# A two-layer hybrid trunk: a new table of start and end positions for the 39 streams that its instructions are woven from

## The chip, the cores and the metric

The kernel runs on one core of one Trainium2 chip, as one program from the input arrays in device memory to the output array. The metric is the device time of an execution in microseconds, the median of several runs; less is better. Besides the times there is a trace of one profiled execution, and all views below are of that one.

The engines are named as in the trace: PE is TensorE's matmuls (PEld its weight loads), DVE is VectorE, ACT is ScalarE, POOL is GpSimd, and SP is the engine that issues the weight loads from device memory. Each engine works through its own list of instructions in order, and waits on semaphores where an instruction needs another engine's result.

## The reference

Two layers. Each normalises x, projects it once to all inputs of four branches, runs the branches, gates each with a SiLU, and maps the four outputs back.

```python
for l in range(DEPTH):                       # DEPTH 2, SEQ 1024, D_MODEL 1024
    h = rms_norm(x, pre_norm_g[l])
    proj = h @ w_in[l]
    (a_val, a_glu, a_gate, b_q, b_f, b_i, b_gate,
     c_xbc, c_dt, c_z, d_cq, d_ckv, d_kr, d_gate) = jnp.split(proj, split_at, axis=-1)
    y_a = conformer_conv_branch(a_val, a_glu, a_gate, ...)   # GLU, causal depthwise conv k=31, LN, swish, pointwise
    y_b = hgrn2_branch(b_q, b_f, b_i, b_gate, ...)           # gated linear recurrence
    y_c = ssd_branch(c_xbc, c_dt, c_z, ...)                  # short conv, chunked scan, gated RMSNorm
    y_d = mla_branch(d_cq, d_ckv, d_kr, d_gate, positions, ...)  # low-rank q / kv, rotary, block-causal attention
    y = jnp.concatenate([y_a, y_b, y_c, y_d], axis=-1) @ w_out[l]
    x = x + rms_norm(y, post_norm_g[l])
```

The depthwise convolution of branch A, `y[t] = sum_k w[k] * h[t-30+k]` per channel over 31 taps, and the recurrence of branch B, `state = exp(b_last) * state + k^T v` with decays inside the chunk, are the two that matter here.

## The kernel before, in words

Everything is in one function, `trunk_kernel`. A layer's body creates some twenty generators, one for each piece of work, and emits their instructions interleaved. In the order in which they come in a layer:

- **v** (`th_v`) projects branch B's values: tiles `psV` (and `psVb` for the first two token blocks of layer 1, whose matmuls follow the previous layer's last blocks as they arrive). PE only waits there for the transposed, normalised input `hh`/`hl`.
- **a** (`th_a`) projects branch A's value and GLU gate (`psA`, each 128 features by 1024 tokens), and DVE multiplies them into the padded inputs `hpad` of the convolution (L468, L470).
- **ca** and **cb** (`th_conv`) are the convolution: 240 instructions `ca<-hpad,col,ca` on DVE (L481), 120 in each layer. They need only `hpad`, their result is read much later (`th_atail`), so they can be put almost anywhere between.
- **fq** (`th_fq`) projects forget gate and query of branch B: `psF`, `psQ`.
- **dt** (`th_dt`) makes branch C's step sizes on DVE, two matmuls `pcs`, a transpose `pct`, and a small transfer of POOL's queue, `acsp<-acT` (L448).
- **b** (`th_b`) is branch B's recurrence. For each half `g` of the tokens there are seven levels, and in each level two halves `m`. A half of a level issues four matmuls `plB` (L625) from `krb` and `qz`, then DVE rescales `qz` (L634) and `krb` (L635) for the next level; after both halves two `copy_predicated` (L648) take the level's `plB` out of PSUM into `amat` (the last two levels use ACT instead). A level's `plB` waits for the last level's L634 and L635. After the levels come `poB`, `ptkB`, `pSB`, which carry the state from block to block.
- **gb**, **gc** (`gate`, tiles `psg`) and **ga**, **gd** (`gate_f`, tiles `psgA`) project the SiLU gates of the branches; POOL's queue stores them (`gsp`, `gspF`) and reads them back later (`gl`, `glA`, `gD`).
- **x** (`th_x`, tiles `psx`) projects branch C's input; DVE does its short convolution (L719). **at** is the rest of branch A, **c** branch C's scan (its `lm` is read by POOL's queue from `acsp`, then gets the mask added by DVE at L736), **d** (`psd`) branch D's projections, **q** and **att** its attention (`psc`, `ptp`, `poD`; DVE's maxima `nm`, ACT's exponentials `pe`).
- **w** (`th_w`) loads the output projection's weights: eight transfers `rawo` through two buffers, each split by ACT into `woh` and by DVE into `wol`. `woh` and `wol` take the room of `hh` and `hl`, so the first split waits for the last matmul that reads `hh`, which is a `psd`. **o** and the code behind it do the output projection (`pz`) and the next layer's normalisation.

A weight chunk from device memory goes through two `raw` buffers, is cut by ACT into a rounded `wh` (L160) and by DVE into the rest `wl` (L176), three buffers each; every product is three matmuls (`wh` by `hh`, `wl` by `hh`, `wh` by `hl`).

What sets the order: each generator has a row (start, end, total) in the table `PLAN`, and is a `Thread` whose position is start + (end - start) * done / total. `weave` always takes the next piece from the thread with the lowest position. The instruction lists that come out of this are then ordered once more at build time by the framework's scheduler, which puts ready instructions ahead; the lists shown below under the change are those that result from both. The positions are numbers on a scale of the table's own; a layer's scale runs to about 505.

Of the kernel before, what the change touches and what calls it, by code (L numbers as in the profile page):

```python
# [43 lines left out]

PLAN = {
    "v0": (-1.1, 7.4, 8),
    "a0": (35.1, 68.9, 41),
    "fq0": (60.4, 110.8, 41),
    "dt0": (104, 115.8, 9),
    "ca0": (53.6, 123, 57),  # L50
    "cb0": (123, 300.5, 63),
    "gb0": (138.1, 155.9, 21),
    "b0": (123.3, 232.4, 120),
    "ga0": (151.5, 181.4, 21),
    "gc0": (203.4, 226.9, 21),
    "gd0": (278.8, 298.3, 21),
    "x0": (220.7, 257, 61.5),
    "at0": (296.3, 363.8, 22),
    "c0": (293.2, 362.4, 48.2),
    "d0": (283.6, 373.2, 72),  # L60
    "q0": (357.3, 375.6, 2),
    "o0": (470, 505, 8.2),
    "rot0": (221.2, 266.5, 1),
    "att0": (347.7, 481.2, 144.8),
    "w0": (425, 460, 8),
    "v1": (-3.5, 30.6, 8),
    "a1": (35.1, 68.9, 41),
    "fq1": (59, 99.6, 41),
    "dt1": (104, 115.8, 9),
    "ca1": (57, 110, 44),  # L70
    "cb1": (110, 284.5, 76),
    "gb1": (117.9, 137.7, 21),
    "b1": (102.3, 200.5, 120),
    "ga1": (130.9, 155.3, 21),
    "gc1": (203.4, 230.3, 21),
    "gd1": (261.8, 280.6, 21),
    "x1": (212.9, 255.7, 61.5),
    "at1": (278.6, 342, 22),
    "c1": (275.5, 340.6, 48.2),
    "d1": (266.1, 351.4, 72),  # L80
    "q1": (335.5, 349.5, 2),
    "o1": (468, 503, 8.2),
    "att1": (347.1, 481.6, 144.8),
    "w1": (425, 455, 8),
}


# [1101 lines left out]
```

## Time and profile before

| | |
|---|---|
| median of 3 runs | 1258.37 us (1258.11 to 1260.59) |
| the profiled execution | 1256.95 us, of which its span is 1255.2 us |
| mean granted TensorE clock | 0.985 of full speed |
| busy over the span: PE, PEld, DVE, ACT, POOL | 1196.8, 985.2, 808.7, 488.5, 180.0 us |
| recurrence of layer 0, from the first `plB` to the last eight | 140.0 to 256.9 us of the span |
| recurrence of layer 1, the same | 752.3 to 873.0 us of the span |

A row of the view by stretches gives, for each engine, its busy microseconds and, in brackets, its instructions; then the clock granted to TensorE as a share of full speed, the busy share of the DMA engines and the GB/s. A row of the timeline gives start, duration, engine, line, operation, the tile written and the tiles read, the count of like instructions that are drawn together, and in square brackets the idle time before it with what ended it. Matmuls overlap in the pipeline, so that the distance from start to start is what one costs, not its duration. A granted clock of 1.00 is 2.4 GHz, 0.50 is 1.2 GHz.

### The profile page before, as it was taken

Reading aid. Unit: us, or ns where it says so; the run is one execution under the profiler, and the core shown is the slowest. Engines: PE = TensorE matmul, PEld = TensorE weight load, DVE = VectorE, ACT = ScalarE, POOL = GpSimd, SP = SyncE. Lnnn points to the kernel's source line nnn. Section 1 sums busy time; section 2 is a strip of 40 time slices with the busy share of each in tenths; the row PEclk is TensorE's granted clock in tenths of the full one; section 3 lists DMA queues with packets and bytes.
Section 4 is the critical chain, followed back from the end, with each engine's and each line's share of the span. In section 5 each row is a group of like instructions: output and inputs, shape, how many; then the busy total and the mean of one; then the engine's idle time right before and its main releaser. Section 6 shows DMA issues by size and latency. Waiting matters only on the chain.

```text
span 1255.2 us, 17851 instructions
## 1 busy us (share of the span) xinstructions
PE 1196.8 (95%) x6902; PEld 985.2 (78%) x6902; DVE 808.7 (64%) x1555; ACT 488.5 (39%) x1112; POOL 180.0 (14%) x290
## 2 busy tenths in 40 slices
PE   5999999999989989999999999998999898999997
PEld 5988899888878846677898889897888696567786
DVE  5566999985366575527454859999763775654432
ACT  5413222233456474425432222322344755643311
POOL 2100011101132111211020001211011232011100
PEclk9999999999989999999999999998999999999999
DMA  8002122211142140234321111211013312111532
GB/s 275 34 34 68 43 85 79 71 41 52 54 134 74 40 154 19 73 125 168 104 94 68 34 51 60 86 59 67 34 49 101 118 60 100 49 40 43 176 138 81
DMA packets 38661, 101.48 MB, mean 81 GB/s; under 512 B 5440, under 2 KB 13808, under 8 KB 38576
## 3 DMA queue, kind: packets, MB, share of 16 engines
q1 hardware_dynamic: 22848, 51.42, 12.1%
q0 software_dynamic: 14864, 46.04, 11.0%
q10 hardware_dynamic: 864, 2.88, 0.6%
q8 instruction: 54, 0.88, 0.3%
q14 instruction: 31, 0.25, 0.1%
HBM read 75.37 MB, written 25.20 MB: 80 GB/s over the span
## 4 chain that ended last, share of the span: by engine, by line
PE 76%; DVE 11%; issue 4%; DMA 4%; ACT 3%; POOL 0%; SPq 0%; DVEq 0%; ACTq 0%; POOLq 0%
PE pz L1012 11%; PE psx L220 4%; PE psx L223 4%; PE psx L226 4%; DVE ca L481 3%; PE poD L949 3%; PE psc L926 3%; PE ptp L944 2%; PE plB L625 2%; PE psA L220 2%; PE psA L223 2%; PE psA L226 2%; PE psgA L347 2%; PE psgA L348 2%; PE psgA L349 2%
## 5 line engine op out<-in xcount | busy, mean ns | idle before, releaser
L481 DVE SCALAR_TENSOR_TENSOR ca<-hpad,col,ca 128x512 f32<-128x512 f32 x240 | 186.1, 781 | 4.0
L176 DVE TENSOR_TENSOR wl<-raw,wh 128x1024 fp32r<-128x1024 f32 (+2 forms) x56 | 66.9, 1194 | 95.3 <-ACT wh L160 95.2
L160 ACT CAST wh<-raw 128x1024 fp32r<-128x1024 f32 (+2 forms) x56 | 57.5, 1027 | 141.5 <-PE psA L223 33.7
L1012 PE MATMUL pz<-woh,yh 128*128 128x512 f32 x240 | 76.9, 400 | 1.2 <-ACT yh L160 1.2
L1012 PE MATMUL pz<-woh,yl 128*128 128x512 f32 x240 | 76.6, 398 | 0.2 <-DVE yl L176 0.2
L1012 PE MATMUL pz<-wol,yh 128*128 128x512 f32 x240 | 76.0, 396 | 0.0
L209 PE MATMUL psg<-wh,hh 128*128 128x256 f32 x256 | 73.9, 289 | 1.5 <-ACT gt L160 1.4
L210 PE MATMUL psg<-wl,hh 128*128 128x256 f32 x256 | 73.2, 286 | 0.0
L211 PE MATMUL psg<-wh,hl 128*128 128x256 f32 x256 | 72.8, 284 | 0.0
L625 PE MATMUL plB<-qz,krb 128*128 128x128 f32 x448 | 62.8, 288 | 8.6 <-DVE krb L635 8.6
L625 PEld LDWEIGHTS plB<-qz,krb 128*128 128x128 f32 x448 | 58.0, 199 | 11.0 <-issue 5.1
L933 ACT ACTIVATE pe<-psc,nm 128x1024 f32<-128x1024 f32 (+7 forms) x64 | 47.1, 738 | 42.6 <-DVE nm L928 22.4
L220 PE MATMUL psx<-hh,wh 128*128 128x512 f32 x192 | 62.8, 406 | 0.0
L223 PE MATMUL psx<-hl,wh 128*128 128x512 f32 x192 | 62.2, 403 | 0.0
L226 PE MATMUL psx<-hh,wl 128*128 128x512 f32 x192 | 61.9, 401 | 0.0
L719 DVE SCALAR_TENSOR_TENSOR xbc<-xpad,col,xbc 128x512 f32<-128x512 f32 x72 | 51.1, 748 | 16.3 <-ACT xbc L172 15.5
L926 PE MATMUL psc<-kT,qTt 96*128 96x512 f32 (+4 forms) x128 | 53.4, 544 | 5.7 <-ACT pe L933 3.5
L1012 PEld LDWEIGHTS pz<-wol,yh 128*128 128x128 f32 x240 | 44.9, 188 | 10.3
L1012 PEld LDWEIGHTS pz<-woh,yl 128*128 128x128 f32 x240 | 44.7, 188 | 10.4 <-DVE yl L176 0.6
L1012 PEld LDWEIGHTS pz<-woh,yh 128*128 128x128 f32 x240 | 44.1, 188 | 10.7 <-ACT yh L160 1.4
L348 PE MATMUL psgA<-hl,wh 128*128 128x512 f32 x128 | 51.0, 398 | 0.0
L347 PE MATMUL psgA<-hh,wh 128*128 128x512 f32 x128 | 50.9, 397 | 0.0
(335 smaller groups left out, 3001.2 us busy)
## 6 DMA issues: line engine op xcount, KB each, us to landing
raw<-in_w_dram SPq DMA_DIRECT2D x44, 512.0 KB, 3.4
rawo<-in_wo_dram SPq DMA_DIRECT2D x16, 512.0 KB, 3.5
gsp<-gt POOLq DMA_DIRECT2D x16, 256.0 KB, 2.5
gl<-gsp POOLq DMA_DIRECT2D x8, 512.0 KB, 5.1
gspF<-gtA POOLq DMA_DIRECT2D x16, 256.0 KB, 2.3
ysp<-gl POOLq DMA_DIRECT2D x8, 512.0 KB, 3.4
lm<-acsp POOLq DMA_DIRECT2D x16, 256.0 KB, 4.0
yt<-ysp SPq DMA_DIRECT2D x16, 256.0 KB, 3.4
```

The source lines that it names most:

```text
L209: T.matmul(ps[:, :n], a, hs[k], start=(k == 0), stop=False)
L210: T.matmul(ps[:, :n], a, ls[k], start=False, stop=False)
L211: T.matmul(ps[:, :n], b, hs[k], start=False, stop=(k == KD - 1))
L220: T.matmul(ps[:, h * 512:(h + 1) * 512], w, hh[:, k, h * 512:(h + 1) * 512], start=(k == 0), stop=False)
L223: T.matmul(ps[:, h * 512:(h + 1) * 512], w, hl[:, k, h * 512:(h + 1) * 512], start=False, stop=False)
L226: T.matmul(ps[:, h * 512:(h + 1) * 512], wl, hh[:, k, h * 512:(h + 1) * 512], start=False, stop=(k == KD - 1))
L347: T.matmul(ps, w, hh[:, k, tk], start=(k == 0), stop=False)
L348: T.matmul(ps, w, hl[:, k, tk], start=False, stop=False)
L481: V.scalar_tensor_tensor(t, hp[:, k:k + 512], w[k], t, op0=ALU.mult, op1=ALU.add)
L625: T.matmul(pl[:, o0:o0 + P].rearrange("p (r b u) -> p r b u", r=2, u=u), k_[:, t_ * P:(t_ + 1) * P], z[:, :, t_ * P:(t_ + 1) * P].rearrang ...
L926: T.matmul(psc[:, c0:c1_], qTt[0:k_, 2 * m + r, :], kT[2 * m + r, c0 // 512][0:k_, 0:c1_ - c0], start=True, stop=True)
L1012: T.matmul(pz[n], a[:, k, :], w[:, k, n * 512:(n + 1) * 512], start=(k == 0 and a is yh and w is wh), stop=(k == KD - 1 and a is yl))
```

## The change

Only the table `PLAN` is replaced: all of its 39 rows but `v0` have other numbers. No instruction is added to or taken from any engine but one more load of an ACT table (23 to 24), and SP's transfers come in the same order. Two rows of each layer, as an example:

```diff
-    "cb0": (123, 300.5, 63),
+    "cb0": (131.0, 304.2, 63),
-    "gb0": (138.1, 155.9, 21),
+    "gb0": (120.6, 156.4, 21),
...
-    "v1": (-3.5, 30.6, 8),
+    "v1": (5.7, 44.5, 8),
-    "a1": (35.1, 68.9, 41),
+    "a1": (13.5, 44.9, 41),
-    "dt1": (104, 115.8, 9),
+    "dt1": (116.3, 159.5, 9),
```

What comes out of it, on the engines concerned:

In layer 1, PE's list where the projection of V goes over from its first two blocks (`psVb`) to the others (`psV`); `psA` are the projections of the convolution branch. Before:

```order
L210 MATMUL psVb_5567<-wl_5561,hh1_4858 128x260
L211 MATMUL psVb_5567<-wh_5560,hl1_4859 128x260
L209 MATMUL psV_5676<-wh_5554,hh1_4858 128x260
L210 MATMUL psV_5676<-wl_5555,hh1_4858 128x260
L211 MATMUL psV_5676<-wh_5554,hl1_4859 128x260
```

Now:

```order
L220 MATMUL psA_5633<-hh1_4858,wh_5623 128x512 x2
L223 MATMUL psA_5633<-hl1_4859,wh_5623 128x512 x2
L226 MATMUL psA_5633<-hh1_4858,wl_5624 128x512 x2
L209 MATMUL psV_5765<-wh_5554,hh1_4858 128x260
L210 MATMUL psV_5765<-wl_5555,hh1_4858 128x260
L211 MATMUL psV_5765<-wh_5554,hl1_4859 128x260
```

Pieces of `psA` now stand in six places between those of V, where before all but 11 matmuls of `psA` followed V.

In layer 1, DVE's list in the last but one level of the recurrence's second half (of seven, both halves `m`): `ca` is the convolution, `qz` and `krb` the rescaling on which the next `plB` waits. Before:

```order
L481 SCALAR_TENSOR_TENSOR ca_7447<-hpad_6103,col_5536,ca_7447 128x512
L634 TENSOR_TENSOR qz_7012<-qz_7012,totB_6334 128x16x32
L635 TENSOR_TENSOR krb_6114<-krb_6114,totB_6334 128x8x32
L481 SCALAR_TENSOR_TENSOR ca_6980<-hpad_6100,col_5536,ca_6980 128x512
L481 SCALAR_TENSOR_TENSOR ca_7447<-hpad_6103,col_5536,ca_7447 128x512
L634 TENSOR_TENSOR qz_7035<-qz_7035,totB_6334 128x16x32
L635 TENSOR_TENSOR krb_6258<-krb_6258,totB_6334 128x8x32
```

Now:

```order
L481 SCALAR_TENSOR_TENSOR ca_6987<-hpad_6015,col_5536,ca_6987 128x512
L634 TENSOR_TENSOR qz_6957<-qz_6957,totB_6328 128x16x32
L635 TENSOR_TENSOR krb_6108<-krb_6108,totB_6328 128x8x32
L481 SCALAR_TENSOR_TENSOR ca_6987<-hpad_6015,col_5536,ca_6987 128x512
L634 TENSOR_TENSOR qz_6969<-qz_6969,totB_6328 128x16x32
L635 TENSOR_TENSOR krb_6250<-krb_6250,totB_6328 128x8x32
```

One `ca` stands there now where two stood. Counted over the whole lists, from the recurrence's first L635 to the one on which its last `plB` waits (142.7 to 250.2 us and 754.8 to 866.7 us before): `ca` 59 before and 46 now in layer 1 (39 and 30 ahead of it, 22 and 44 behind it), 53 and 45 in layer 0 (51 and 60 ahead, 16 and 15 behind); `wl` 6 and 4, `prB` 3 and 2, the L607 rows 6 and 4 in each layer; and five small rows of `th_dt` and one of `th_c` (L437, L438, L443, L447, L777) come into it in each layer. On PE, from first to last `plB`: `psg` 384 and 358, `psx` 24 and 2, `dsB` 24 and 32 in layer 0; `psg` 384 and 374, `psx` 19 and 2 in layer 1; `pcs` and `pct` come in.

In layer 1, PE's list at the handover to the attention: the last `psd` (after which `wol` may be written), then the first scores `psc`. Before:

```order
L832 MATMUL psd_9051<-idn_81,cn_9077 128x128 x3
L760 MATMUL pyC_9094<-xdt_9018,lm_8986 128x64 x4
L764 MATMUL pyC_9094<-hst_8200,xbc4_7897 128x128
L764 MATMUL pyC_9094<-hst_8200,xbc5_7966 128x128
L872 MATMUL pq_9114<-qbt_5542,cqT_8050 128x384
L872 MATMUL pq_9114<-qbt_5542,cqT_8051 128x384
L847 MATMUL pk_9153<-kvt_5543,ckT_9090 128x512
L860 MATMUL pk_9133<-idn_81,kk_9135 96x128 x4
L885 MATMUL ptq_9125<-idn_81,qk_9117 96x128 x4
L860 MATMUL pk_9153<-idn_81,kk_9155 96x128 x4
L926 MATMUL psc_9184<-kT_8042,qTt_9040 128x512
```

Now:

```order
L832 MATMUL psd_9089<-idn_81,cn_9115 128x128 x3
L847 MATMUL pk_9133<-kvt_5543,ckT_9017 128x512
L847 MATMUL pk_9153<-kvt_5543,ckT_9128 128x512
L860 MATMUL pk_9133<-idn_81,kk_9135 96x128 x4
L860 MATMUL pk_9153<-idn_81,kk_9155 96x128 x4
L926 MATMUL psc_9184<-kT_8116,qTt_9043 128x512
```

The scan's `pyC` and the queries' `pq` and `ptq` stand ahead of the last `psd` now. In layer 0 it is alike: `pyC`, `pq` and one `ptq` went ahead of it.

On POOL's queue in layer 1, `acsp<-acT` stood ahead of all stores of the gate `gb`; now it stands behind the second store of `gc`, near the recurrence's end, and the first `lm<-acsp` one store behind it. On DVE the mask addition to that `lm` (L736) then comes between the last two L635 of the recurrence.

## Rows read from the trace of the kernel before

**Rows 1.** The page's first section: busy time and share of the span.
```profile
PE 1196.8 (95%) x6902; PEld 985.2 (78%) x6902; DVE 808.7 (64%) x1555; ACT 488.5 (39%) x1112; POOL 180.0 (14%) x290
```

**Rows 2.** View by stretches of 25 us: PE, PEld, DVE, ACT, POOL; clock, DMA.
```profile
100.00:125.00 25.00, 25.00 (x112) 20.41 (x111) 14.66 (x29) 9.35 (x15) 0.00 (x0) 1.00 0.18 63
...
225.00:250.00 25.00, 21.97 (x178) 21.20 (x177) 24.87 (x45) 7.10 (x14) 6.05 (x6) 0.92 0.22 74
...
325.00:350.00 25.00, 25.00 (x112) 20.66 (x111) 6.54 (x9) 10.90 (x17) 4.34 (x8) 1.00 0.25 84
...
850.00:875.00 25.00, 19.44 (x109) 17.23 (x108) 24.96 (x40) 5.67 (x11) 2.86 (x3) 0.80 0.22 75
...
975.00:1000.00 25.00, 20.82 (x133) 17.67 (x132) 17.90 (x62) 19.38 (x64) 6.85 (x12) 1.00 0.40 123
```

**Rows 3.** The same columns for the recurrences, and for the stages beside layer 1's.
```profile
140.00:256.90 116.90, 112.94 (x834) 105.40 (x834) 115.29 (x194) 29.70 (x57) 20.19 (x26) 0.97 0.21 73
142.70:250.20 107.50, 103.54 (x788) 97.40 (x788) 106.27 (x184) 29.70 (x57) 18.31 (x24) 0.98 0.21 74
752.30:873.00 120.70, 113.26 (x830) 105.27 (x830) 118.89 (x200) 29.67 (x58) 20.12 (x25) 0.96 0.19 71
754.80:866.70 111.90, 104.46 (x789) 97.73 (x789) 110.14 (x188) 29.65 (x57) 18.73 (x24) 0.97 0.21 76
...
686.50:754.80 68.30, 68.30 (x312) 55.73 (x311) 47.72 (x84) 16.08 (x23) 0.53 (x1) 1.00 0.14 47
875.00:975.00 100.00, 99.91 (x486) 82.15 (x485) 56.90 (x89) 40.35 (x66) 12.45 (x21) 1.00 0.20 64
```

**Rows 4.** DVE's groups by line in 754.8 to 866.7: count, busy us, mean ns, idle.
```profile
L481 DVE SCALAR_TENSOR_TENSOR ca<-hpad,col,ca 128x512 f32<-128x512 f32 x59 | 45.4, 778 | 0.7
...
L176 DVE TENSOR_TENSOR wl<-raw,wh 128x1024 fp32r<-128x1024 f32 x6 | 7.3, 1213 | 0.0
...
L607 DVE TENSOR_TENSOR qz<-qp,fg 64x512 f32<-64x512 f32 x6 | 4.1, 683 | 0.0
...
L598 DVE TENSOR_TENSOR prB<-qp,krb 128x512 f32<-128x512 f32 x3 | 2.0, 686 | 0.0
```

**Rows 5.** Timeline of PE at the end of layer 1's recurrence.
```profile
859.49 1.34 PE L625 MATMUL plB<-qz,krb 128*128 128x128 f32 x8 [3.45 <-DVE krb L635]
...
869.43 1.05 PE L220 MATMUL psx<-hh,wh 128*128 128x512 f32 x2
...
872.95 1.05 PE L625 MATMUL plB<-qz,krb 128*128 128x128 f32 x8
```

**Rows 6.** Timeline of PE in layer 0's recurrence, two neighbouring gate matmuls.
```profile
206.75 0.28 PE L209 MATMUL psg<-wh,hh 128*128 128x256 f32 x1
206.87 0.28 PE L210 MATMUL psg<-wl,hh 128*128 128x256 f32 x1
```

**Rows 7.** View by stretches: the two handovers to the attention.
```profile
437.20:459.70 22.50, 17.24 (x73) 8.88 (x73) 19.02 (x31) 19.26 (x39) 4.54 (x6) 1.00 0.55 188
1053.50:1075.90 22.40, 17.89 (x62) 9.07 (x61) 17.82 (x31) 18.25 (x38) 4.81 (x6) 0.85 0.49 165
```

**Rows 8.** Timeline of PE at layer 1's handover.
```profile
1053.66 1.00 PE L760 MATMUL pyC<-xdt,lm 128*128 128x64 f32 x8
...
1056.79 1.12 PE L847 MATMUL pk<-kvt,ckT 128*128 128x512 f32 x2 [0.33 <-DVE cqT L160]
...
1062.63 6.59 PE L926 MATMUL psc<-kT,qTt 100*128 100x512 f32 x8 [1.10 <-ACT kT L160]
```

**Rows 9.** What reads `rawo`: count, min/median/max ns, first and last start.
```profile
L176 DVE TENSOR_TENSOR wol<-rawo,woh x8: 1212/1221/1226, 437.2 to 1061.8; 128x1024 fp32r<-128x1024 f32 x8
```

**Rows 10.** Transfers from POOL's queue: count, KB each, median us to landing.
```profile
gsp<-gt POOLq DMA_DIRECT2D x16, 256.0 KB, 2.5
...
gspF<-gtA POOLq DMA_DIRECT2D x16, 256.0 KB, 2.3
...
lm<-acsp POOLq DMA_DIRECT2D x16, 256.0 KB, 4.0
```

More of the change, by code (lines that the diff above doesn't have):

```diff
@@ L46 @@
     "v0": (-1.1, 7.4, 8),
[L47 to L50, printed above, removed]
-    "cb0": (123, 300.5, 63),
-    "gb0": (138.1, 155.9, 21),
[L53 to L58, printed above, removed]
-    "c0": (293.2, 362.4, 48.2),
[L60 to L65, printed above, removed]
-    "v1": (-3.5, 30.6, 8),
-    "a1": (35.1, 68.9, 41),
-    "fq1": (59, 99.6, 41),
-    "dt1": (104, 115.8, 9),
[L70 to L84, printed above, removed]
+    "a0": (34.2, 67.6, 41),
+    "fq0": (104.3, 116.8, 41),
+    "dt0": (124.5, 129.4, 9),
+    "ca0": (56.5, 116.0, 57),
+    "cb0": (131.0, 304.2, 63),
+    "gb0": (120.6, 156.4, 21),
+    "b0": (120.8, 230.5, 120),
+    "ga0": (156.4, 186.3, 21),
+    "gc0": (205.1, 219.6, 21),
+    "gd0": (273.1, 274.1, 21),
+    "x0": (216.6, 270.4, 61.5),
+    "at0": (296.3, 361.6, 22),
+    "c0": (293.2, 362.4, 48.2),
+    "d0": (302.0, 372.7, 72),
+    "q0": (360.0, 385.0, 2),
+    "o0": (474.0, 507.1, 8.2),
+    "rot0": (235.4, 295.8, 1),
+    "att0": (356.5, 493.5, 144.8),
+    "w0": (435.6, 485.6, 8),
+    "v1": (5.7, 44.5, 8),
+    "a1": (13.5, 44.9, 41),
+    "fq1": (51.5, 90.6, 41),
+    "dt1": (116.3, 159.5, 9),
+    "ca1": (54.2, 116.7, 44),
+    "cb1": (116.2, 280.3, 76),
+    "gb1": (117.8, 125.5, 21),
+    "b1": (99.5, 192.9, 120),
+    "ga1": (118.3, 173.6, 21),
+    "gc1": (182.3, 209.6, 21),
+    "gd1": (257.3, 280.3, 21),
+    "x1": (201.8, 233.0, 61.5),
+    "at1": (281.5, 341.5, 22),
+    "c1": (259.4, 326.1, 48.2),
+    "d1": (266.1, 356.4, 72),
+    "q1": (331.2, 342.1, 2),
+    "o1": (462, 503, 8.2),
+    "att1": (352.9, 480.9, 144.8),
+    "w1": (430, 455, 8),
 }
```

## The prediction

> **What bounds the kernel now.** I read the busy shares first, then the span in stretches of 25 us, then each stretch in which PE is idle or its clock is down. PE is busy for 95% of the span [rows 1], so the kernel is PE's, and a new order can only win what PE loses to waits and to half clock. These losses are few and stand together: the ends of both recurrences (225 to 250 us and 850 to 875 us: PE 21.97 and 19.44 of 25 at 0.92 and 0.80 of the clock), the start of branch C's scan (975 to 1000 us: 20.82) [rows 2], and the handovers to the attention (17.24 of 22.5 and 17.89 of 22.4) [rows 7]. The reader is to look at DVE in the same rows: at the ends of the recurrences it is full (24.87 of 25).
>
> So over the recurrences DVE is the bound. From the first `krb` to the one on which the last `plB` waits it is busy 106.27 of 107.5 us in layer 0 and 110.14 of 111.9 us in layer 1 [rows 3]. PE runs ahead while it has gate matmuls to put between, and then stands: at the end of layer 1 it waits 3.45 us for a `krb`, and the matmuls behind that run at half clock: two `psx` of 512 columns take 1.05 us [rows 5], where the stretch 325 to 350 us has 112 matmuls of mostly that size in 25.00 us, 0.223 each [rows 2]. A fall of the clock to 1.2 GHz follows the wait, so the wait is paid twice.
>
> **The change, part by part.**
>
> *DVE in the recurrences.* Between the same two `krb`, layer 1 loses 13 `ca` at 0.778, 2 `wl` at 1.213, one `prB` at 0.686 and 2 L607 at 0.683 [rows 4]: 10.1 + 2.4 + 0.7 + 1.4 = 14.6 us. Five small rows come in; no row here gives their price, which lies between nothing and that of an L607 each (3.4 us together). They are of 32 columns, mostly, so I take 1 us. DVE's need falls from 111.9 to 98.3 us. In layer 0 it is 8 `ca`, 6.2 us, and the rest alike: 10.7 - 1 = 9.7, from 107.5 to 97.8 us.
>
> *PE in the recurrences.* A gate matmul costs 0.12 us from start to start [rows 6], a `psx` 0.223. Layer 1 gives up 10 `psg` and 17 `psx`: 1.2 + 3.8 = 5.0 us. Layer 0 gives up 26 and 22, 3.1 + 4.9, and gets 8 `dsB`, which I take at the 0.1 of the gates: 7.2 us. This work isn't gone, PE does it before or behind at full speed, so it is a debt against any gain. What PE would need: its busy 113.26 us in layer 1 at a clock of 0.96 is at most 113.3 - 4.8 = 108.5 us at full clock (0.04 of 120.7 us given back), less 5.0 is 103.5. In layer 0 it is 112.94 - 3.5 - 7.2 = 102.2 us [rows 3].
>
> *The new length.* DVE's side: 2.5 to 2.7 us from first `plB` to first `krb` [rows 3], then 98.3 (97.8), then about 1 us to the last `plB`, since the 19 to 24 `psx` that stood in its way (6.3 and 6.7 us, partly at half clock) are 2 now: 102 us in each layer. PE's side is 102 to 103.5. With both near 102 neither can be followed without a gap; I take 104, with 102 and 108 as bounds. The stretch to the last `plB` was 120.7 and 116.9 us. Gain in layer 1: 120.7 - 104 - 5.0 = 11.7 us; in layer 0: 116.9 - 104 - 7.2 = 5.7 us. Bounds: each 2 us better, 4 worse.
>
> *Where the `ca` go.* Layer 0 has 9 more ahead of its recurrence, 7 us, where DVE had 14.66 of 25 us busy in the stretch before it [rows 2]: hidden. Layer 1 has 22 more behind, 17 us, in a stretch of 100 us with 56.9 us of DVE work at full PE [rows 3]: 74 of 100, hidden, and if it weren't, `psx` would wait for DVE's short convolution to free its PSUM, us for us.
>
> *The start of layer 1.* `psA` amid V brings the first `hpad` earlier on PE, but DVE works in order and now has the `wl` of later chunks ahead of the first `ca`, which wait for weight buffers that V holds until its last matmul. I put the first `ca` some 20 us later than the 686.5 us of now. In 686.5 to 754.8 us DVE is busy 47.72 of 68.3 us [rows 3]; 9 `ca` less leave 40.7 for the 48 us that remain. So it fits by 2 to 7 us. Cost: nothing, with the rival below.
>
> *The handover.* `wol` can be written only behind the last `psd`, and its eight pieces, of 1.22 us on DVE [rows 9] with ACT's splits and transfers between, fill the two stretches of 22 us in which PE loses 5.3 and 4.5 us [rows 7]. The work behind the last `psd` covers the beginning: 1053.66 to 1062.63 us, 9.0 us with 3.2 us of waits in it, so 5.8 of work [rows 8]. Now only four groups of `pk` are left, about 2.4 us; `pyC`, `pq` and `ptq` come before, and the chain starts 3.4 us later against the work. Nothing hides that if the chain sets the end of the stage, all of it does if not: 0 to 3.4 us each. As DVE and ACT are busy for 18 to 19 us of the 22 [rows 7], I take 3 us, in both layers: 6 us lost.
>
> *The scan of layer 1.* Gate `psgA` pieces stand between the steps of the scan now, where PE lost 4.2 us in 975 to 1000 us [rows 2]. Bounds 0 and 4; I take 2 us won. In layer 0 nothing of the kind stands out: 0.
>
> *POOL's queue.* The first `lm` is asked for late, behind a gate store, and DVE's L736 between the last two `krb` waits for it. From that store's gate matmuls to the last `plB` PE has some 6.5 us of work by the prices above, and the transfer takes 4.0 us [rows 10] besides two issues: 0 to 2 us of wait on DVE, which `psx` covers on PE (22 of them, 5 us). Cost nothing.
>
> Transfers of POOL's queue don't suffer from a full DVE: the stores `gsp` all fall in the recurrences and land in 2.5 us, the stores `gspF` of the same size, half of them outside, in 2.3 us [rows 10]. The Trainium skill, "SBUF — State Buffer", section "SBUF: two separate sides", speaks against this part of the change: the descriptors of such a transfer are written by GpSimd through a port pair that it shares with DVE, and that some DVE operations hold for their whole length, so that the transfer starves. By that rule `lm` would come late; the rows differ by 0.2 us.
>
> **The sum.** 11.7 + 5.7 - 6 + 2 = 13.4 us. The profiled execution took 1256.95 us, which gives 1243.6; the median of the runs lies 1.4 us above, and from it the time is 1258.37 - 13.4 = 1245.0 us.
>
> **The rivals.**
>
> *Lockstep.* DVE and PE now both need about 102 of 104 us in the recurrences, and each half level hands over twice. If the gaps add up to the upper bound of 108 us in each layer, the gain is 8 us less, and less still if the scan gives nothing: about 1253 us. For it: PE waits 3.45 and DVE is full at the end of layer 1 although only DVE is short there [rows 5]. Against it: DVE's rows have next to no idle time before them [rows 4], so it finds work while it waits for PE.
>
> *Slower: DVE late into layer 1's recurrence.* If the first `ca` comes much more than 20 us late, the `ca` whose place in the list is ahead of the first `krb` push the recurrence back, us for us beyond the 2 to 7 us of slack, and PE has at that point only one gate's matmuls in hand. From a start about 18 us later still it would eat the whole gain; 25 us more than I put would give 1245 + 20 = 1265 us. For it: in the list nothing of the convolution can go past the `wl` that wait. Against it: what is left of V then, 144 matmuls at about 0.12 us, is 17 us of work, and `psA` between makes it at most twice that.
>
> *`lm` late.* If that transfer took 10 us in place of 4, DVE would stand 5 us behind the last `krb` but one, with `ptkB` and the state behind it: 1250 us. The rule of the Trainium skill's page "SBUF — State Buffer" named above would bring this.
>
> *The change doesn't do what it says.* Waits move but their number stays, the clock falls as often: then the recurrences give about as much as the handovers take, 1258 us.
>
> **How the numbers follow.** The forecast, 1245 with its own bounds (4 better in the recurrences and 3 at a handover, 8 worse), has 0.64; lockstep 0.15; `lm` 0.05; nothing changed 0.06; late DVE 0.10. The range leaves out 2 in 10: the slower case, half of the unchanged one, and the far end of what is better, 1235 to 1256. A measurement of this kernel tells about 0.2%, 2.5 us, from no change. Faster by more: 0.64 + 0.15 + 0.05 = 0.84, of which the last two lose 0.01; same 0.06; slower 0.10, with 0.01 more.
>
> **What would show it.** Right: the stretch from first to last `plB` is 102 to 108 us in both layers, PE waits little for `krb`, and no half clock stands at the recurrences' ends; DVE is near full there still. The handovers lose about 3 us more PE time each. Wrong: a gap on PE before the first `plB` of layer 1 or between its first levels (late DVE); DVE idle before L736 (`lm`); waits on `krb` spread over all levels (lockstep); or no loss at all at the handovers, in which case the time is lower by up to 6 us.

## The result, and the profile after

The changed kernel takes 1243.57 us (median of 4 runs, 1242.19 to 1244.76) against 1258.98 us for the kernel before in the same session: a ratio of 0.9876, 95% interval 0.986 to 0.9893, 15.4 us. The forecast was 1245.0 us. The profiled execution took 1244.03 us, its span is 1242.3 us. One execution of the run that spreads the splits in the kernel before was slow (1971.17 us at a mean granted clock of 0.557); the figures of that run below are those of the other three.

The first section of the page after, to be read beside [rows 1]: PE is busy 3.7 us less, of a span that is 12.9 us shorter.

```profile
PE 1193.1 (96%) x6902; PEld 980.4 (79%) x6902; DVE 806.7 (65%) x1555; ACT 490.6 (39%) x1113; POOL 181.0 (15%) x290
```

Stretches of 25 us after, with the columns of [rows 2]: the recurrences' ends (225 to 250 and 825 to 850 us; the last eight `plB` start at 244.2 and 850.4 us), the 25 us before the second of them, and the start of the scan in layer 1.

```profile
225.00:250.00 25.00, 25.00 (x196) 24.06 (x195) 24.93 (x41) 8.07 (x16) 6.62 (x7) 1.00 0.24 86
...
800.00:825.00 25.00, 25.00 (x171) 21.92 (x170) 24.66 (x46) 5.70 (x10) 2.34 (x6) 0.93 0.19 68
825.00:850.00 25.00, 25.00 (x217) 24.99 (x216) 24.28 (x46) 8.57 (x19) 6.93 (x8) 1.00 0.27 92
...
950.00:975.00 25.00, 22.94 (x139) 20.50 (x140) 18.37 (x55) 18.66 (x53) 6.84 (x13) 0.97 0.46 148
```

Where PE had 21.97 and 19.44 of 25 us at 0.92 and 0.80 of the clock, at the recurrences' ends, it has all of it at 1.00. DVE is as full as before. The recurrences from the first `plB` to the last eight, and the two handovers in 25 us from the last `psd` matmul that reads `hh` or `hl`, after:

```profile
140.30:244.20 103.90, 102.69 (x799) 96.88 (x798) 101.89 (x181) 29.03 (x57) 19.74 (x25) 1.00 0.21 75
744.50:850.40 105.90, 105.63 (x808) 99.29 (x808) 103.78 (x184) 30.07 (x59) 19.57 (x27) 0.98 0.22 76
...
427.60:452.60 25.00, 20.79 (x80) 10.62 (x79) 18.46 (x31) 20.55 (x38) 2.40 (x4) 0.86 0.50 169
1036.50:1061.50 25.00, 18.30 (x53) 8.35 (x52) 15.27 (x24) 18.24 (x35) 1.29 (x3) 0.80 0.37 126
```

The recurrences went from 116.9 to 103.9 and from 120.7 to 105.9 us [rows 3]; PE is idle for 1.2 and 0.3 us of them. The handover of layer 1 got worse: 6.7 of 25 us idle, the clock at 0.80. PE's waits for `krb`, before and after, with the total, the count and the longest:

```profile
PE plB L625 <- DVE krb L635: 8.6, 6, 3.4
...
PE plB L625 <- DVE krb L635: 0.3, 1, 0.3
```

What was waited for most inside the recurrence is down to 0.3 us, and a wait of 3.0 us is new. It stands in front of the transposes that end layer 1's `psd`. The timeline there, PE first, then DVE:

```profile
1040.69 0.55 PE L832 MATMUL psd<-idn,cn 128*128 128x128 f32 x3 [2.96 <-DVE krd L160]
...
1047.71 5.40 PE L926 MATMUL psc<-kT,qTt 100*128 100x512 f32 x8 [0.68 <-ACT kT L160]
1055.01 3.54 PE L926 MATMUL psc<-kT,qTt 100*128 100x512 f32 x4 [1.90 <-ACT pe L933]
```

```profile
1037.98 2.36 DVE L176 TENSOR_TENSOR wol<-rawo,woh 128x1024 fp32r<-128x1024 f32 x2
1040.26 0.28 DVE L160 COPY kT<-pk 96x128 f32<-96x128 f32 x1
1040.46 0.18 DVE L160 COPY krd<-psd 128x32 f32<-128x32 f32 x1
```

Two `wol` splits, 2.36 us, stand ahead of the copy that empties the last `psd`, and PE's transposes wait for that copy.

### The profile page after: what moved, and what is told of

Read it like the earlier page. It is cut to its first block, busy times and chain, and to the rows that moved or that the text cites. A ratio compares the mean times of both kernels' runs of the same rounds, so it can differ in the third digit from the quotient of the medians.

```text
span 1242.3 us, 17842 instructions
## 1 busy us (share of the span) xinstructions
PE 1193.1 (96%) x6902; PEld 980.4 (79%) x6902; DVE 806.7 (65%) x1555; ACT 490.6 (39%) x1113; POOL 181.0 (15%) x290
## 5 line engine op out<-in xcount | busy, mean ns | idle before, releaser
L326 POOL DMA_DIRECT2D gsp<-gt x16 | 11.7, 734 | 280.2 <-ACT gt L325 270.1
```

## The experiments

All are tables or small edits of the two kernels. Where two numbers of a stage are compared, they are rows of the view by stretches from the same first to the same last instruction.

**One layer alone.** The table of before, with the 19 rows of layer 1 replaced:

```diff
-    "v1": (-3.5, 30.6, 8),
+    "v1": (5.7, 44.5, 8),
...
-    "w1": (425, 455, 8),
+    "w1": (430, 455, 8),
```

> Table of before with the rows of layer 1 alone replaced. If the two layers add up, layer 1's recurrence takes 105.9 us from first to last eight plB as in the changed kernel (120.7 before), its handover loses as much as there, layer 0 is as before, and the time is 1249 to 1252 us. If the layers depend on one another (the end of layer 0 sets what layer 1 can do), the time is off that by more than 2 us.

1247.64 us against 1258.3 (0.992, interval 0.9894 to 0.9945). Layer 0's recurrence is as long as before, layer 1's as in the changed kernel:

```profile
141.80:258.10 116.30, 112.64 (x834) 105.97 (x834) 114.91 (x194) 29.72 (x57) 20.17 (x26) 0.97 0.22 74
752.10:857.90 105.80, 105.55 (x806) 99.22 (x807) 103.65 (x184) 29.99 (x59) 19.48 (x27) 0.98 0.22 76
```

Alone, the rows of layer 1 bring 10.7 us, which leaves 4.7 of the 15.4 us to layer 0; each of the two figures is uncertain by 3 to 4 us, going by the intervals. The prediction's sum, taken by layers, had 11.7 + 2 - 3 = 10.7 and 5.7 - 3 = 2.7. The stages of the changed kernel's own trace divide it otherwise: its last `ptp` of layer 0 stands at 539.1 us in place of 545.9, so that 6.8 us of the span's 12.9 are won up to there and 6.1 behind it. So how much each layer brings in the changed kernel is not settled by these runs. The time is 1.4 us under the range that was expected; the stretches are as expected.

**DVE or PE as the bound.** A table that thins DVE only in layer 1, and PE in both:

```diff
-    "b0": (123.3, 232.4, 120),
+    "b0": (120.8, 230.5, 120),
...
-    "b1": (102.3, 200.5, 120),
+    "b1": (99.5, 192.9, 120),
...
-    "gb1": (117.9, 137.7, 21),
+    "gb1": (117.8, 125.5, 21),
```

(and `x`, `ca`, `cb`, `gb`, `ga`, `gc` of both layers).

> Table of before with the rows of the recurrence, of branch C's projection, of the convolution and of three gates replaced. In layer 0 DVE keeps its 53 ca, 6 wl and 3 prB in the recurrence while PE loses 24 psg and 10 psx of it (5.1 us); in layer 1 DVE has 46 ca and 4 wl. DVE as the bound: layer 0's stretch stays at 113 to 117 us although PE has 5 us less to do, layer 1's falls to 103 to 107 us. PE's filling as the bound: layer 0's stretch falls by 5 us or more to under 112, as layer 1's.

```profile
144.40:259.50 115.10, 107.79 (x809) 100.56 (x808) 113.44 (x193) 29.77 (x57) 20.09 (x25) 0.99 0.22 74
766.70:873.10 106.40, 101.70 (x783) 95.27 (x784) 103.90 (x180) 25.47 (x51) 18.12 (x24) 1.00 0.18 65
```

In layer 0 PE's busy time fell by 5.1 us, from 112.94, and the stretch by 1.8 us only: PE waits more. DVE is busy for 113.44 of 115.1 us; its own work fell from 115.29 us, by as much as the stretch. In layer 1, with 13 `ca` less, it is 106.4 us. So in layer 0 the length follows DVE and not PE; in layer 1 both have less to do. The whole is slower than before, 1263.86 us (1.0037, 1.0021 to 1.0053): what layer 1's recurrence wins is lost elsewhere. In layer 0 the scan, from its first `pstC` to the last `psd`, takes 80.6 us (365.4 to 446.0) where it took 74.6 (360.5 to 435.1), and the attention behind it 114.5 (446.0 to 560.5) where it took 110.8. Why these rows of the table do that alone was not followed up.

**Less work for DVE.** The kernel before, with half the columns of each tap in layer 1; its result lacks the other half of these sums.

```diff
-                        V.scalar_tensor_tensor(t, hp[:, k:k + 512], w[k], t, op0=ALU.mult, op1=ALU.add)
+                        c_ = 256 if l == 1 else 512
+                        V.scalar_tensor_tensor(t[:, 0:c_], hp[:, k:k + c_], w[k], t[:, 0:c_], op0=ALU.mult, op1=ALU.add)
```

> The kernel before; in layer 1 each tap of the convolution is added for 256 of its 512 columns only, so part of that layer's output is left out. DVE as the bound of the recurrence: DVE's work there falls by some 20 us, below PE's, and the stretch from first to last eight plB falls from 120.7 to 100 to 104 us with few waits on krb. The recurrence's own chain (plB, qz, krb, next level) as the bound: the stretch stays above 112 us, with waits on krb in every level.

```profile
750.50:854.20 103.70, 102.31 (x795) 96.42 (x796) 101.65 (x203) 26.77 (x53) 17.95 (x23) 1.00 0.20 70
```

The stretch falls from 120.7 to 103.7 us, the time to 1245.51 us (0.9917, 0.989 to 0.9944). The edit touches DVE alone, but in the order that results 15 `psg` and 18 `psx` leave the stretch too, 5.8 us by the prediction's prices. That leaves 11.2 us won, and the time fell by 10.7. The same edit in the changed kernel:

> The changed kernel; in layer 1 each tap of the convolution is added for 256 of its 512 columns only, so part of that layer's output is left out. DVE has some 20 us less in layer 1's recurrence and PE 45 gate matmuls less (5.4 us). If DVE still sets the changed kernel's recurrence, PE's loss there falls well below its 6.7 us, to 3 or less. If PE's own work is the bound by now, the loss stays at 5 to 7 us and the stretch falls by the 5 us of PE work alone, to about 100 us.

```profile
745.30:845.20 99.90, 98.53 (x760) 92.19 (x760) 96.03 (x195) 28.26 (x56) 19.16 (x24) 1.00 0.20 70
```

6.0 us shorter than the changed kernel's 105.9, of which PE's 45 gate matmuls less, at 0.12 us, are 5.4. PE idles 1.4 us here, 0.3 us there, and the clock is 1.00 in place of 0.98. So PE's own work is the bound of the changed kernel's recurrence in layer 1, and to thin DVE further gives next to nothing. (Its time, 1248.69 us median, scatters from 1241.88 to 1250.15 and says little; its profiled execution, with 1241.88, is the lowest.)

**What stands ahead of the recurrence.** The changed kernel with three rows of layer 1 as before:

```diff
-    "v1": (5.7, 44.5, 8),
-    "a1": (13.5, 44.9, 41),
-    "fq1": (51.5, 90.6, 41),
+    "v1": (-3.5, 30.6, 8),
+    "a1": (35.1, 68.9, 41),
+    "fq1": (59, 99.6, 41),
```

> The changed kernel with three rows of layer 1 as before (V, branch A's projection, forget gate and query): psA stands behind V again, 39 ca ahead of the recurrence, 47 in it, 34 behind. If the gain of layer 1 is the ca taken out of the recurrence and what was moved ahead of it does not matter, the stretch is 103 to 107 us and the time within 3 us of 1243.6. If psA amid V brings a gain of its own, the time is above 1247 us.

1251.53 us, 0.9967 of the kernel before in its session (0.9951 to 0.9983): most of the gain is gone, and the second of the two expectations came. By the profiled spans it is 7.6 us (1249.9 and 1242.3), by the two ratios 11.4. The stretch, and DVE at its start:

```profile
745.80:855.60 109.80, 104.12 (x787) 97.45 (x788) 106.31 (x186) 28.42 (x56) 19.55 (x26) 0.98 0.19 68
```

```profile
748.18 0.42 DVE L635 TENSOR_TENSOR krb<-krb,fg 128x256 f32<-128x256 f32 x1
...
749.30 0.69 DVE L598 TENSOR_TENSOR prB<-qp,krb 128x512 f32<-128x512 f32 x1
749.91 1.38 DVE L607 TENSOR_TENSOR qz<-qp,fg 64x512 f32<-64x512 f32 x2
...
757.71 0.42 DVE L635 TENSOR_TENSOR krb<-krb,fg 128x256 f32<-128x256 f32 x1
```

The same rows in the changed kernel:

```profile
745.64 0.68 DVE L598 TENSOR_TENSOR prB<-qp,krb 128x512 f32<-128x512 f32 x1
746.25 1.38 DVE L607 TENSOR_TENSOR qz<-qp,fg 64x512 f32<-64x512 f32 x2
...
748.26 0.42 DVE L635 TENSOR_TENSOR krb<-krb,fg 128x256 f32<-128x256 f32 x1
...
752.32 0.41 DVE L635 TENSOR_TENSOR krb<-krb,fg 128x256 f32<-128x256 f32 x1
```

The stretch is 3.9 us longer than in the changed kernel with 20 gate matmuls, 2.4 us, less in it. The second half of the first level (`prB`, L607) comes behind the first `krb`, and the second `krb` 9.5 us behind the first. In the changed kernel these rows stand ahead of the first `krb`, and the second follows after 4.1 us. So the three rows together are worth several microseconds: with them the first level's inputs are done before the recurrence begins. The run doesn't separate V and A interleaved from the third row, which starts forget gate and query earlier, though `prB` and L607 read `qp` and `fg`, which come from these. Nor was it separated whether the early inputs, or the one `ca` more and the 2.1 us of `prB` and L607 in the recurrence, weigh more.

**The handover: the order of the splits.** The changed kernel, the first two `wo` splits put behind the copies that empty the last `psd`:

```diff
+                if k < 2:
+                    behind_(h_, marks["a"][0])
+                    behind_(l_, marks["v"][0])
```

(`behind_` sets an order on one engine, as `in_order` does; `h_`, `l_` are the two splits, `marks` the copies to `cn` and `krd`.)

> The changed kernel, with the first two wo splits put behind the last psd's copies on ACT (cn) and DVE (krd). If the splits that stand ahead of these copies cost the 3.0 us of the wait before layer 1's last psd transposes, that wait is under 1 us and the time falls by 2 to 4 us, to 1240 to 1242. If PE only lacks work there, the wait moves to pk or psc and the time stays at 1243 to 1244 us.

```profile
1041.24 0.55 PE L836 MATMUL psd<-idn,cn 128*128 128x128 f32 x3 [0.73 <-DVE krd L160]
...
1052.57 6.00 PE L930 MATMUL psc<-kT,qTt 100*128 100x512 f32 x8 [3.43 <-ACT kT L160]
1062.37 2.07 PE L930 MATMUL psc<-kT,qTt 100*128 100x512 f32 x2 [3.80 <-ACT pe L937]
```

The wait of 2.96 us is 0.73, and 1250.44 us is slower than the changed kernel: the splits come later, as packed as before, and now delay ACT's `kT` copies and the first exponentials. My theory of the one copy fell. It is not one wait, it is eight splits in a row on two engines that work in order. And the splits are not only work: ACT also stands still in front of them until their weights have landed, with the exponentials behind. ACT's waits for these transfers in the changed kernel:

```profile
ACT woh L976 <- DMA rawo<-in_wo_dram: 3.1, 3, 1.4
...
ACT woh L160 <- DMA rawo<-in_wo_dram: 1.6, 2, 0.8
```

These are 4.7 us in both layers together, and 6.7 us in this run.

**The handover: the splits spread.** In the changed kernel each split is tied behind every second exponential (ACT) and the maximum beside it (DVE):

```diff
+                behind_(h_, marks["pe"][2 * k])
+                behind_(l_, marks["nm"][min(2 * k + 1, len(marks["nm"]) - 1)])
```

> The changed kernel, with the eight wo splits of a layer tied one by one behind the exponentials and maxima of the first four blocks of attention. If the chain of the wo splits on ACT and DVE is what PE loses to in the 25 us behind the last psd (4 us in layer 0, 7 us and half clock in layer 1), 5 to 9 us come back: 1235 to 1239 us. If the attention's own chain (scores, maximum, exponential, next scores) sets these stages, 0 to 2 us: 1242 to 1244.

1231.45 us (0.9793, 0.9771 to 0.9814), 12.1 us under the changed kernel, 10.4 by the two ratios, and more than the 5 to 9 us that were expected. The 25 us behind the last `psd`:

```profile
429.60:454.60 25.00, 22.48 (x114) 12.77 (x113) 14.49 (x33) 17.77 (x38) 2.28 (x4) 1.00 0.19 64
1033.10:1058.10 25.00, 22.61 (x115) 12.69 (x114) 15.12 (x30) 18.09 (x40) 1.46 (x3) 1.00 0.13 43
```

PE has 22.48 and 22.61 us where it had 20.79 and 18.30, and full clock. ACT's waits for `rawo` are gone. Whether the splits' work or these waits weighed more was not separated. The same edit on the kernel before:

> The kernel before, with its wo splits spread over the first four blocks of attention as in w_spread. If the packed splits cost the same with the old cover as with the new, this gains the 12 us that w_spread gained on the changed kernel: 1246 us. If the old cover hid part of them, as the prediction had it, it gains 3 us less in each layer: 1250 to 1253 us.

1244.06 us against 1256.21 (0.9907, 0.9878 to 0.9936), 12 us: within the runs' scatter as much as on the changed kernel. So the old cover did not hide the packed splits. Rows from the last `psd` to the last `ptp` of layer 0 and layer 1; before and after the change with packed splits:

```profile
435.10:545.90 110.80, 103.95 (x682) 69.04 (x681) 63.96 (x133) 59.23 (x135) 17.12 (x25) 1.00 0.22 70
1051.40:1165.00 113.60, 106.62 (x683) 70.24 (x682) 64.88 (x133) 59.15 (x135) 17.56 (x25) 0.97 0.18 58
```

```profile
427.60:539.10 111.50, 104.46 (x668) 68.63 (x666) 61.80 (x127) 58.04 (x129) 14.97 (x23) 0.97 0.21 69
1036.50:1151.20 114.70, 104.95 (x663) 68.23 (x662) 61.11 (x123) 57.81 (x130) 14.25 (x22) 0.96 0.16 53
```

and with spread splits, first on the kernel before, then on the changed one:

```profile
431.80:537.80 106.00, 102.64 (x683) 69.50 (x681) 64.92 (x134) 57.98 (x135) 17.42 (x26) 1.00 0.23 74
1043.50:1149.80 106.30, 102.89 (x683) 69.43 (x682) 64.74 (x133) 58.26 (x135) 17.54 (x26) 1.00 0.20 63
```

```profile
429.60:535.50 105.90, 100.99 (x666) 67.80 (x664) 61.01 (x127) 57.66 (x129) 14.86 (x23) 1.00 0.23 73
1033.10:1138.00 104.90, 100.12 (x663) 66.96 (x661) 60.78 (x123) 56.92 (x130) 14.19 (x22) 1.00 0.18 58
```

How much work left the stage with the change is read where the clock is full in all rows, with spread splits: PE is busy for 1.7 us less in layer 0 (102.64 and 100.99) and 2.8 us less in layer 1 (102.89 and 100.12). In layer 0 that is `pyC` and one group of `pcb`, 16 matmuls, and not the 3.4 us that the prediction priced for both layers. With packed splits the stage is even 0.7 and 1.1 us longer: 2.4 and 3.9 us lost. With spread splits it is 0.1 and 1.4 us shorter: 1.6 and 1.4 us lost, with no packed chain to blame.

**The cover put back.** The changed kernel with the rows of branch D, queries, attention and `wo` as before:

```diff
-    "d1": (266.1, 356.4, 72),
-    "q1": (331.2, 342.1, 2),
+    "d1": (266.1, 351.4, 72),
+    "q1": (335.5, 349.5, 2),
```

(and the like of `att1`, `w1`, and of layer 0.)

> The changed kernel with the rows for branch D's projection, the queries, the attention and wo as before in both layers. In layer 0 the work behind the last psd is that of before again (pyC, pq, pk, ptq), in layer 1 only pk and ptq, no pyC. If the missing cover is what the handovers lose, 3 us come back in layer 0 and 1 to 3 in layer 1: 1238 to 1240 us. If the packed splits are what PE waits for whatever stands there, the time stays within 2 us of 1243.6.

The times don't settle it: 1244.39 us median of five that lie between 1238.86 and 1248.32. The same with `d` and `q` alone, on top of the spread splits:

> w_spread with the rows of branch D's projection and of the queries as before, in both layers. Layer 0's last psd has pyC, pq, pk and ptq behind it again, layer 1's only pk and ptq. If the missing cover costs its 2.5 to 3 us apart from the packed splits, layer 0's loss behind the last psd falls by that and the time is 1227 to 1229.5 us. If with the splits spread nothing is left for the cover to hide, it stays at 1230.5 to 1232.5 us.

1228.38 us (0.9763, 0.9743 to 0.9783): 3.1 us under w_spread, and 31.6 us under the kernel before of its session. It is the best version of the study. The time is in the range that was expected of a cover that counts, but the trace doesn't show that the cover made it, and the intervals of the two ratios overlap. From the first `plB` of a layer to its last `ptp`, where the changed rows are at work, w_spread first:

```profile
141.70:535.50 393.80, 383.11 (x2418) 315.88 (x2416) 277.33 (x585) 171.92 (x410) 72.44 (x109) 1.00 0.22 72
742.90:1138.00 395.10, 385.76 (x2435) 317.06 (x2434) 297.25 (x606) 179.29 (x415) 71.50 (x108) 1.00 0.20 69
```

```profile
140.90:534.70 393.80, 383.47 (x2418) 315.88 (x2416) 277.52 (x584) 171.71 (x410) 72.81 (x109) 1.00 0.22 72
740.50:1135.80 395.30, 386.51 (x2435) 318.30 (x2434) 297.27 (x606) 179.41 (x415) 71.84 (x108) 1.00 0.21 69
```

Both layers are as long as in w_spread. The 3.1 us lie ahead of these stretches (0.8), between them (1.6, with the clock at 1.00 in place of 0.98) and behind them (0.9), where the two kernels have the same rows. So what the missing cover costs by itself stays open.

**Spread wider.** Each split behind every third exponential, with the table's `w` rows later to match.

> w_spread with the splits spread wider, each behind every third exponential in place of every second. If ACT and DVE are still too full in the first blocks of attention, 1 to 3 us more come back: 1228.5 to 1230.5. If the attention's own chain is what is left, or the last splits come late for the output projection, 1231 to 1234 us.

1238.65 us, 7 us slower than every second. Part of it is where the last splits are needed, from the last `ptp` to PE's last matmul: 88.4 us with PE busy 83.95, where w_spread has 84.4 and 82.29.

```profile
1143.30:1231.70 88.40, 83.95 (x372) 67.45 (x371) 27.97 (x34) 19.04 (x45) 5.50 (x10) 0.98 0.40 134
```

```profile
1138.00:1222.40 84.40, 82.29 (x371) 66.19 (x371) 27.95 (x34) 19.04 (x45) 5.53 (x10) 1.00 0.42 141
```

## Why the prediction was right, point by point

**The recurrences.** The first step was DVE's need between two `krb`, 98.3 and 97.8 us. Measured from start to start it is 98.8 us in layer 1, from 748.26 to 847.09 us in DVE's timeline of the changed kernel, which follows at the recurrence's start and end, and 99.1 us in layer 0 (142.65 to 241.74 us); DVE is busy for 97.35 and 97.15 us of them.

```profile
744.50 1.22 DVE L176 TENSOR_TENSOR wl<-raw,wh 128x1024 fp32r<-128x1024 f32 x1 [4.08 <-ACT wh L160]
...
748.26 0.42 DVE L635 TENSOR_TENSOR krb<-krb,fg 128x256 f32<-128x256 f32 x1
```

```profile
847.09 0.41 DVE L635 TENSOR_TENSOR krb<-krb,totB 128x256 f32<-128x256 f32 x1
...
852.16 0.68 DVE L736 TENSOR_TENSOR lm<-lm,negb 128x512 f32<-128x512 f32 x1
```

The second step was PE's side, 103.5 us in layer 1 and 102.2 in layer 0 at full clock. PE is busy for 105.63 us at a clock of 0.98, which is 103.5 by the prediction's own conversion, and for 102.69 us at 1.00. The stretches were put at 104 and are 105.9 and 103.9 us. What layer 1 has beyond 104 is the clock: it is 0.93 in 800 to 825 us, where PE's row shows no idle time, and the prediction had falls of the clock behind waits only. That DVE was the bound is shown from both sides, by b_new and half_ca1. That PE is the bound now in layer 1, after_half_ca1 shows. Lockstep, the first rival, didn't come: PE waits 0.3 us for `krb`.

**DVE late into layer 1.** The first `ca` starts at 701.6 us, 15 us later than before, where 20 was put. The first `krb` comes 3.8 us behind the first `plB` in place of 2.5. It isn't the `ca`: DVE stands 4.08 us for ACT's `wh` of the next weight chunk, as the row above shows, and then `prB` and the two L607, 2.1 us, stand ahead of `krb` and no longer behind it. No run shows that this costs anything, as PE has 0.3 us of idle time in the whole stretch. "Cost: nothing" holds, but the prediction did not see what the start is worth: va_back, with the rows for V, A, forget gate and query as before, loses 7.6 us by the spans. The sum had that gain in the recurrence's terms, by counting the rows that the list has there, without seeing which rows of the table bring it.

**`lm`.** The last row above has no wait in brackets: the transfer was there. It was issued at 845.0 us, while DVE was full, and landed 3.9 us later. The rival fell. The Trainium skill's page "SBUF — State Buffer", section "SBUF: two separate sides", has it that such a transfer starves while some DVE operations run; this trace shows no such delay, and whether the operations that fill DVE here are of that kind was not tested.

**The handovers.** 3 us each was forecast; 2.4 and 3.9 are measured, and 1.6 and 1.4 with the splits out of the way. The size is right in the mean of the two layers, but the price of 3.4 us behind it was too high for layer 0, where 1.7 us of work left the stage. The mechanism is half shown: part of the loss stays without a packed chain, so that it isn't all because the chain of splits starts later against the work; the rest, 0.8 and 2.5 us, may be that, and was not separated. What I had not priced, since the change doesn't touch it, is the chain itself: 10 to 12 us in either kernel.

**The scan.** 2 us were put for layer 1. In 25 us at its start PE has 22.94 us at a clock of 0.97 where it had 20.82 at 1.00. From the recurrence's end to the last `psd`, before and after:

```profile
873.00:1051.40 178.40, 173.12 (x921) 144.62 (x919) 108.07 (x263) 84.08 (x215) 33.60 (x57) 1.00 0.21 67
```

```profile
850.40:1036.50 186.10, 182.62 (x967) 152.65 (x966) 132.79 (x300) 92.19 (x227) 37.72 (x60) 0.99 0.21 70
```

PE's idle time there fell from 5.3 to 3.5 us, by 1.8, about what was put; but the clock is 0.99 in place of 1.00. The stage grew by 7.7 us, and the work that came into it is 5.0 us from the recurrence, by the prediction's price, and 2.8 from behind the last `psd`, by the rows of the handover: of the 2 us next to nothing is left. For layer 0 "nothing of the kind stands out: 0" was a misreading. In the 25 us in which its scan starts (350 to 375 us) PE had 21.29 us at a clock of 0.87, and has 21.67 at 1.00. The scan's own row, `c0`, is unchanged, as `v0` is.

**The sum.** 13.4 us were forecast, 15.4 are measured, 12.9 by the two profiled spans. By the stages of these spans layer 0 gave 6.8 us where its terms had 2.7, and what is behind it 6.1 where the terms of layer 1 had 10.7. So the total is nearer to the forecast than its parts by layer, and that is in part luck.

## What to carry to other kernels

Where two engines hand work to and fro in a loop, count what each has to do between two fixed instructions of the loop, in the order that is really issued; the longer of the two counts is the loop, and the work that is only filling (here a convolution) is what to move. Before work is moved away from a place, ask what it hides there: 1.7 and 2.8 us of cover went ahead of the last projection here, and the stage that had held it got 0.7 and 1.1 us longer. And look for bursts of independent work that stand in front of a chain on engines that work in order: tied one by one behind the chain's own steps, the eight splits of each layer cost 10 to 12 us less in all, while two of them pushed back, with the rest as packed as before, cost more. The burst here stood in front of the chain with its work and with the transfers that it waits for.

## What the runs showed of the hardware that was not expected

TensorE's granted clock doesn't go by the idle time of a stretch alone. In the handover of layer 1 the mean is 0.80 in 25 us with 6.7 us idle, and 1.00 with 2.4 us idle when the splits are spread. But in the kernel before, the handover of layer 0 had 5.3 of 22.5 us idle at 1.00 [rows 7], and in the changed kernel the clock is 0.93 in 800 to 825 us, where PE's row shows no idle time; the fall stands at 806 us, behind 3 us of matmuls that are 2 and 64 columns wide (`dsB`, `poB`, `pSB`). So a wait can cost more than its own length, as at the end of layer 1's recurrence before the change, and from its length alone these traces don't tell whether it will.
